# Second pairs of the second matrices in seven products on six input tiles, with two weight sums by adding transfers

## The chip, the core and the metric

One core of a Trainium2 chip. The time is the device time of one execution, in microseconds. A profiled execution leaves a trace of every instruction on each engine: PE (TensorE), DVE (VectorE), ACT (ScalarE), POOL (GpSimd), and SP, which only issues transfers. The matmuls' weight loads appear as a row of their own, PEld.

## What is computed

A trunk of two layers on 256 tokens of width 2048, in float32. Layer one: norm, one projection to queries, keys, values and forget gates, attention with a decaying bias, output projection, then an MLP with squared ReLU. Layer two takes shared keys and values from the residual stream, attends in chunks with a learned relative bias, and has an MLP of its own. The part that the change concerns above all is the MLP:

```python
def sq_relu_mlp(h, g, w1, w2):
    a = jax.nn.relu(rms_norm(h, g) @ w1)      # 2048 -> 8192
    return (a * a) @ w2                       # 8192 -> 2048
```

It is computed once in each layer, with h of 256 x 2048.

## The kernel before

**Units.** All weights stream from HBM once, as units of 128 x 1024 float32 (512 KB): two input tiles (of 128 rows) by 512 output columns. The token side stands on PE as 128 x 128 pieces, so a product of one input tile, 512 columns and 128 tokens is one matmul position. A float32 product is made from three passes of a shorter format. ACT rounds a unit to a high part (`hi`, line 184), DVE subtracts it to get the low part (`lo`, line 185), and PE adds high times high (line 408), high weight times low token part (line 410) and low weight times high token part (line 412). A plain unit is 2 input tiles x 2 token blocks x 3 passes = 12 matmuls.

**Queues.** Each engine works its instructions in the order in which the program writes them (`keep_order` at the end fixes it for DVE, ACT, PE and SP). `load` issues the transfer of a unit on SP into one of four `raw` buffers; `issue` writes its split on ACT and DVE; `fetch` keeps three split units ahead of PE and three loaded ones ahead of these. `hi` and `lo` have three buffers each. Everything else, such as transposes, norms, softmax and ReLU, is put in small steps into `fill`, one list of steps being run after each plain unit.

**Pairs.** An MLP is cut into four chunks of 2048 hidden columns. In each, two pairs of the first matrix and two of the second are computed; a pair is two panels (a and b) of 512 output columns over 16 input tiles. The first four input tiles of a pair are done with seven products instead of eight: with the two token blocks and the two panels they form a 2 x 2 by 2 x 2 product of blocks, and Strassen's method in Winograd's form needs seven block products on sums of blocks. The four weight blocks are called 11, 12, 21 and 22; the sums T1 = 12 - 11, T3 = 22 - 12, T2 = T3 + 11 and T4 = 21 - T2 are made on DVE from units in SBUF (`make`, line 760). The sums on the token side (`sums`, line 230) are made once for each input of a pair. The seven products, called forms f0 to f6, use 11, T3, T2, T1, 21, T4 and 22 in this order (`class Form`), 6 matmuls each (`form_products`). Copies and additions in PSUM (lines 837, 845, 853, 856) bring the partial results to where the remaining twelve plain units of the pair, a2 to a7 and b2 to b7, go on adding. Forms and plain units alternate by a written plan (`plan_mlp`), the first three forms with b5, b6 and b7 of the pair before.

**Weights of a pair's forms.** `prepare` brings the four blocks by SP (`bring`, line 744) and makes T1 and T3 a stated number of plain units before the pair begins (`Pair.units`). The blocks live in the rooms that keys and values have in attention (tags k and v, two buffers each), T1 and T3 in the room of the attention bias (tag bias, two buffers of 128 x 1536); T2 takes 12's place and T4 takes 11's.

**Around the change.** The first products need part of x (`load_x`, line 72, four tiles a transfer) and the first weights. The forget gates are summed, written to DRAM (`cd`, line 695) and read back broadcast as the bias of the first attention (`decay_bias`, line 712), both issued by SP; the second attention reads its relative bias in `rel_bias`, line 889.

Of the kernel before, what the change touches and what calls it, by code (L numbers as in the profile page):

```python
# [31 lines left out]
REL = 384  # L32

# [13 lines left out]
def trunk(ctx: ExitStack, tc: tile.TileContext, xT, xr, gs, hg, bf, wgate, w_in, w_oa, w1a, w2a,  # L47
          w_kv, w_qb, w_ob, w1b, w2b, rel, out):
# [23 lines left out]
    def load_x(i):  # L72
        raw_x[i] = qkv.tile([P, GH, T], F32, name="xin", tag="kv"[i // 2], bufs=2)
        SY.dma_start(raw_x[i], xT[:, i * GH : (i + 1) * GH, :])
# [3 lines left out]
    load_x(0)  # L78

# [4 lines left out]
    ones = const.tile([P, T], F32, name="ones")  # L84
    V.memset(ones, 1.0)
    warm = ps_o.tile([P, 512], F32, name="pt", tag="po")
    for _ in range(11):
        TE.matmul(warm[:, :P], ones[:, :P], ones[:, :P], start=True, stop=True)
# [18 lines left out]
    class Form:  # L107

        def __init__(self, pair, i):
            self.pair, self.name = pair, ("11", "T3", "T2", "T1", "21", "T4", "22")[i]  # L110
# [8 lines left out]
    class Pair:  # L119
# [3 lines left out]
        def __init__(self, src, first, order, third):  # L123
            self.src = [[src[first + q * 8 + u] for u in range(8)] for q in range(2)]
            self.third, self.ps, self.t, self.room, self.units = third, None, {}, None, (9, 8, 7, 6, 5, 2)
            self.head = {"early": "a2 f4 a3 f5 b2 f6 b3 a4 b4 a5 a6 a7", "late": "a2 f4 a3 f5 b2 f6 b3 a4 a5 b4 a6 a7",
                         "": "a2 f4 a3 f5 a4 f6 a5 a6 a7 b2 b3 b4"}[order]

        def items(self, names):
            return [(self, "abf".index(i[0]), int(i[1])) for i in names.split()]  # L130

    def plan_mlp(w1, w2, tail):
        n, pairs = w1.shape[0] // NCH, []
        for c in range(NCH):
            for src, late in ((w1, ""), (w2, "late")):
                for q in range(2):
                    pairs.append(Pair(src, c * n + 16 * q, (late if pairs else "early") if q == 0 else "", len(pairs) % 2 == 0))
        pairs[0].units, pairs[1].units, pairs[2].units = (15, 13, 11, 8, 10, 8), (9, 8, 7, 6, 3, 2), (9, 8, 7, 6, 1, 2)
        plan, rest = [], [(tail, 0, u) for u in range(KT // UA - 3, KT // UA)]
        for p in pairs:  # L140
            f = p.items("f0 f1 f2 f3")
            plan += [f[0], rest[0], f[1], rest[1], f[2], rest[2], f[3]] + p.items(p.head)
            rest = p.items("b5 b6 b7")
        plan += rest
        units.extend(Form(p, i) if q == 2 else p.src[q][i] for p, q, i in plan)
        return plan
# [6 lines left out]
    plan_a = plan_mlp(w1a, w2a, tail_a)  # L153
# [5 lines left out]
    plan_b = plan_mlp(w1b, w2b, tail_b)  # L159
# [15 lines left out]
    def issue(parts=1):  # L175
        if not raws:
            load(parts)
        raw, cuts = raws.popleft()
        if not cuts:
            raw, cuts = raw.pair.t[raw.name], [slice(0, UN)]  # L180
        hi = wsp.tile([P, UN], F32R, name="hi")
        lo = wsp.tile([P, UN], F32R, name="lo")
        for c in cuts:
            S.activation(hi[:, c], raw[:, c], AF.Copy)  # L184
            V.tensor_tensor(lo[:, c], raw[:, c], hi[:, c].bitcast(F32), op=ALU.subtract)  # L185
        ready.append((hi, lo))

    def fetch(ahead=AHEAD, early=EARLY):
        while (units or raws) and len(ready) <= ahead:
            issue()  # L190
        while units and sum(1 for r in raws if r[1]) < early:
            load()
        return ready.popleft()
# [36 lines left out]
    def sums(a, fs):  # L230

        w = [wk.tile([P, 512], F32, name="sum", tag="wk") for _ in range(2)]

        def part(i):
            v = w[i // 2][:, i % 2 * 256 : i % 2 * 256 + 256].rearrange("p (g t) -> p g t", g=2)
            return v.rearrange("p g (i c) -> p g i c", i=4) if len(a[0][0].shape) == 4 else v

        V.tensor_tensor(part(0), a[1][0], a[1][1], op=ALU.add)
        V.tensor_tensor(part(1), part(0), a[0][0], op=ALU.subtract)
        V.tensor_tensor(part(2), a[0][0], a[1][0], op=ALU.subtract)  # L240
        V.tensor_tensor(part(3), a[0][1], part(1), op=ALU.subtract)
        hi, lo = ([fs[k][:, i * 512 : (i + 1) * 512] for i in range(2)] for k in range(2))
        for i in range(2):
            S.activation(hi[i], w[i], AF.Copy)
        yield
        for i in range(2):
            V.tensor_tensor(lo[i], w[i], hi[i].bitcast(F32), op=ALU.subtract)
        yield

    def split_turned(t, n, which, into, fs=None):  # L250
        x = acts.tile([P, 2, GH, T], F32R, name="act")
        y = qkv.tile([P, GH, REL], F32, name="bias")[:, :, :T]
# [45 lines left out]
    def turned(name="q"):  # L298
        z = qkv.tile([P, GH * T], F32, name="z")
        return z, qkv.tile([P, GH * T], F32, name=name, tag=name, bufs=2)  # L300


    LONG = ((0, 1, 3, 5, 9, 10, 13, 14), (0, 1, 3, 5, 11, 12), (0, 1, 3, 5, 9, 10), (0, 1, 3, 5, 9, 10))
    SHORT = ((3, 1, 2, 3, 6, 7, 9, 10), (4, 2, 3, 5, 10, 11), (1, 2, 3, 4, 9, 10), (0, 0, 1, 2, 4, 5))

    def next_x(n, r2, stats, which, into, kept=None, fs=None, then=None):
# [21 lines left out]
        def f(b, ps):  # L328
            add_h(b, ps)
            if b == NB - 1:  # L330
                step = steps(use)
                do = [rows, turn, lambda: way[0](), lambda: way[1](), step, step, step, step]
                items = [[] for _ in range(max(at) + 1)]
                for i, d in zip(at[: 6 if fs is None else 8], do):
# [18 lines left out]
    class RowStats:  # L353
# [27 lines left out]
        def spread(self):  # L381
            self.R = const.tile([P, T], F32, name="R")
            pr = ps_o.tile([P, 512], F32, name="pt", tag="po")
            rb = wk.tile([P, NB, P], F32, name="rb", tag="wk")
            for b in range(NB):
                V.tensor_scalar(rb[:, b], ones[:, :P], self.r[:, b : b + 1], None, op0=ALU.mult)
# [48 lines left out]
    def form_products(ps, hi, lo, x, fs, i):  # L435
        items = []
        for g in range(2):
            if i in (0, 4, 5):
                xp = [x[2 * g + (i > 0)][:, k, (i == 5) * P : (i == 5) * P + P] for k in range(2)]
            else:  # L440
                c = {3: 0, 2: 1, 1: 2, 6: 3}[i] * 256 + g * P
                xp = [fs[k][:, c : c + P] for k in range(2)]
            items.append((ps[i not in (4, 5)][i in (1, 5)], xp, g, i < 2 and g == 0, i < 2 and g == 1))
# [177 lines left out]
    def begin(u):  # L621
        if u == 0:
            load(2)
            load(2)
# [24 lines left out]
    wgr = const.tile([P, KT * H], F32, name="wgr")  # L649
    ct = {}  # L650

    def gates(x, st):
# [5 lines left out]
        def clear():  # L658
            G.memset(w.bitcast(F32), 0.0)

# [11 lines left out]
        c = const.tile([H, T], F32, name="gc")  # L672

        def logs():
# [14 lines left out]
            V.tensor_tensor_scan(c, ones[:H, :], z, 0.0, op0=ALU.mult, op1=ALU.add)  # L689
# [5 lines left out]
            SY.dma_start(ct["cd"], nct)  # L695
            yield

        def turn_c():
            pc = ps_o.tile([P, 512], F32, name="pt", tag="po")
            ct["cq"] = const.tile([P, NB, H], F32, name="cq")  # L700
            for b in range(NB):
# [5 lines left out]
                [step], [step], [step], [step], [], [turn_c]]  # L707

    def decay_bias(g, box):
        nb = qkv.tile([P, GH, REL], F32, name="bias")  # L710
        src = ct["cd"][g * GH : (g + 1) * GH, :]
        SY.dma_start(nb, src.unsqueeze(0).to_broadcast([P, GH, REL]))
# [10 lines left out]
    for g in range(NG):  # L723
# [12 lines left out]
        zk, k = turned("k")  # L736
        v = qkv.tile([P, NB, 512], F32, name="v")
# [4 lines left out]
    def bring(p, name):  # L742
        t = qkv.tile([P, UN], F32, name="w" + name, tag="kv"[name[1] == "2"], bufs=2)
        SY.dma_start(t, p.src[int(name[1]) - 1][int(name[0]) - 1])
        p.t[name] = t

    def make(p, name):
        t = p.t
        if name in ("T1", "T3"):
            if p.room is not None:  # L750
                t[name] = p.room[:, (name == "T3") * UN : (name == "T3") * UN + UN]
            else:
                t[name] = qkv.tile([P, GH * REL], F32, name="w" + name, tag="bias", bufs=2)[:, :UN]
        elif name == "T2":
            t[name] = t["12"]
        else:
            t[name] = t["11"]
        a, b, op = {"T1": ("12", "11", ALU.subtract), "T3": ("22", "12", ALU.subtract),
                    "T2": ("T3", "11", ALU.add), "T4": ("21", "T2", ALU.subtract)}[name]
        V.tensor_tensor(t[name], t[a], t[b], op=op)  # L760

    def prepare(p, d):
        if d == p.units[0] and p.units[0] > 9:
            p.room = prob.tile([P, 9 * 3 * P], F32, name="wTT", tag="p", bufs=1)
        for name, at in zip(("12", "11", "22", "21", "T1", "T3"), p.units):
            if d == at:
                (make if name[0] == "T" else bring)(p, name)

    def mlp(plan, x, Sx, st, last):
# [4 lines left out]
        def take(t, c, n):  # L774
# [14 lines left out]
            if c or n:  # L789
                low()  # L790
                yield
            if n == 0:
                room = prob.tile([P, 9 * 3 * P], F32R, name="Sh", tag="p", bufs=1)
                Sh[c].extend(room[:, i * GH * T : (i + 1) * GH * T] for i in range(2))
                yield from sums([[t3[:, 2 * j + b :: 4] for j in range(2)] for b in range(NB)], Sh[c])
                if not c:
                    low()
                    yield

        def turn_hidden(c, n, late):  # L800
            zt = []

            def f(b, ps):
                if b == 0:
                    zt.extend(turned())
                blocks32(ps, zt[0], b)
                if b == NB - 1:
                    step = steps(lambda: take(zt[1], c, n))
                    uses = (4, 5, 6, 6 if late else 7) if n % 2 else (4, 5, 7, 8, 9, 10)[: 6 if n == 0 else 4]
                    if not c and n < 2:  # L810
                        uses = (5, 6, 7, 8) if n else (4, 5, 6, 7, 8, 10)
# [5 lines left out]
        def open_pair(p):  # L817
# [6 lines left out]
            else:  # L824
                p.evac = [turn_hidden(c, 2 * r + q, r == 1) for q in range(2)]

        starts = [i for i, it in enumerate(plan) if it[1:] == (2, 0)]
        for i, (p, q, u) in enumerate(plan):
            hi, lo = fetch()
            if p.ps is None:  # L830
                open_pair(p)
            if q == 2:
                form_products(p.ps, hi, lo, p.x, p.fs, u)
                if u == 0:
                    make(p, "T2")
                if u == 2:
# [138 lines left out]
```

## Time and profile before

| what | before |
|---|---|
| median of 3 runs | 2109.74 us (2108.97 to 2109.75) |
| the profiled execution, its own time | 2109.01 us |
| its span, first to last instruction | 2107.2 us |
| granted TensorE clock, mean | 1.000 |
| matmuls | 9332 |
| read from HBM | 450.01 MB |
| transfers under SP's queue | 489.96 MB, 71.2% of 16 engines' span |

The span is what the trace covers; the time has about 1.8 us around it. Busy times are of one engine; several work at once, so they don't add up to the span. A row of the groups reads: line, engine, operation, output and inputs, shapes, count, then total busy time and mean duration in ns, then the idle time before the group and what ended it. A row of the timeline reads: start, duration, engine, line, operation, count, and in brackets how long the engine had been idle and who released it.

### The profile page before, as it was taken

What the parts mean: (1) busy time and instruction counts of PE and PEld (TensorE: products, weight loads), DVE (VectorE), ACT (ScalarE), POOL (GpSimd) and SP (SyncE); (2) the same over time, 40 slices, a digit from 0 to 9 for tenths busy, and PEclk for the clock granted to TensorE, in tenths of its full rate; (3) what the DMA queues carried; (4) which work ended last, traced back from release to release, by engine and by line L of the source; (5) the groups of instructions that cost most, each with busy time, mean ns of one, the idle gap of its engine ahead of it and who ended that gap; (6) DMA issues with size and microseconds to landing.
All of it is one profiled execution on the core that took longest, in us unless ns stands there. A gap on an engine that the chain in (4) does not pass through costs nothing.

```text
span 2107.2 us, 26036 instructions
## 1 busy us (share of the span) xinstructions
PE 2099.1 (100%) x9332; PEld 1741.2 (83%) x9332; DVE 1587.3 (75%) x1812; ACT 1191.4 (57%) x1431; POOL 48.7 (2%) x47
## 2 busy tenths in 40 slices
PE   9999999999999999999999999999999999999999
PEld 8788888888888888888888888888888888888887
DVE  6777676887788777778767677678877877887775
ACT  6545455665466565556575455456654654665653
POOL 1001000000000000000001000000000000000000
PEclk9999999999999999999999999999999999999999
DMA  8787778776676676577678777787766666766774
GB/s 289 236 257 231 234 250 272 241 238 231 216 241 212 211 250 230 188 245 259 194 242 259 238 233 233 227 279 240 257 227 202 232 230 217 236 216 210 244 239 146
DMA packets 182594, 491.63 MB, mean 233 GB/s; under 512 B 36784, under 2 KB 74048, under 8 KB 182464
## 3 DMA queue, kind: packets, MB, share of 16 engines
q1 hardware_dynamic: 182464, 489.96, 71.2%
q8 instruction: 73, 1.20, 0.2%
q14 instruction: 57, 0.47, 0.1%
HBM read 450.01 MB, written 39.87 MB: 232 GB/s over the span
## 4 chain that ended last, share of the span: by engine, by line
PE 99%; DMA 1%; SPq 0%; ACT 0%; DVE 0%; issue 0%; DVEq 0%; ACTq 0%
PE acc L408 26%; PE acc L410 26%; PE acc L412 26%; PE s L408 6%; PE s L412 6%; PE s L410 6%; DMA raw<-in_w_in 1%; PE po L581 1%; PE s L550 1%; PE po L582 0%; PE s L549 0%; PE s L670 0%; DMA turn<-z 0%; SPq L294 0%; ACT hi L184 0%
## 5 line engine op out<-in xcount | busy, mean ns | idle before, releaser
L185 DVE TENSOR_TENSOR lo<-raw,hi 128x1024 fp32r<-128x1024 f32 (+1 forms) x642 | 778.3, 1216 | 296.8 <-ACT hi L184 286.5
L184 ACT ACTIVATE hi<-raw 128x1024 fp32r<-128x1024 f32 (+1 forms) x642 | 677.6, 1057 | 515.2 <-PE acc L410 394.7
L408 PE MATMUL acc<-hi,act 128*128 128x512 f32 x2306 | 632.9, 393 | 2.9 <-ACT hi L184 2.9
L410 PE MATMUL acc<-hi,act 128*128 128x512 f32 x2306 | 623.8, 389 | 0.0
L412 PE MATMUL acc<-lo,act 128*128 128x512 f32 x2306 | 623.5, 389 | 0.0
L410 PEld LDWEIGHTS acc<-hi,act 128*128 128x128 f32 x2306 | 432.8, 188 | 90.4
L412 PEld LDWEIGHTS acc<-lo,act 128*128 128x128 f32 x2306 | 432.8, 188 | 89.9
L408 PEld LDWEIGHTS acc<-hi,act 128*128 128x128 f32 x2306 | 430.8, 188 | 90.9 <-ACT hi L184 3.8
L184 ACT ACTIVATE hi<-w 128x1024 fp32r<-128x1024 f32 x160 | 169.5, 1059 | 153.8 <-PE acc L410 94.4
L185 DVE TENSOR_TENSOR lo<-w,hi 128x1024 fp32r<-128x1024 f32 x160 | 194.8, 1218 | 69.3 <-ACT hi L184 68.3
L408 PE MATMUL s<-hi,act 128*128 128x512 f32 x448 | 121.1, 389 | 0.0
L410 PE MATMUL s<-hi,act 128*128 128x512 f32 x448 | 121.0, 389 | 0.0
L412 PE MATMUL s<-lo,act 128*128 128x512 f32 x448 | 121.0, 389 | 0.0
L184 ACT ACTIVATE hi<-wT 128x1024 fp32r<-128x1024 f32 x60 | 63.6, 1059 | 62.1 <-PE acc L410 41.6
L410 PEld LDWEIGHTS s<-hi,act 128*128 128x128 f32 x448 | 84.1, 188 | 17.5
L412 PEld LDWEIGHTS s<-lo,act 128*128 128x128 f32 x448 | 84.1, 188 | 17.5
L408 PEld LDWEIGHTS s<-hi,act 128*128 128x128 f32 x448 | 84.0, 188 | 17.4
L185 DVE TENSOR_TENSOR lo<-wT,hi 128x1024 fp32r<-128x1024 f32 x60 | 73.2, 1220 | 28.0 <-ACT hi L184 27.8
L760 DVE TENSOR_TENSOR wT<-w,w 128x1024 f32<-128x1024 f32 x60 | 73.1, 1218 | 0.0
L584 ACT ACTIVATE act<-po 128x256 fp32r<-128x256 f32 x32 | 12.3, 385 | 91.1 <-PE po L582 91.1
L492 POOL TENSOR_TENSOR rn<-vv,mhalf 128x4 f32<-128x4 f32 x32 | 43.3, 1366 | 389.9 <-DVE vv L491 389.7
L585 DVE TENSOR_TENSOR act<-po,act 128x256 fp32r<-128x256 f32 x32 | 13.6, 425 | 51.3 <-ACT act L584 51.3
(164 smaller groups left out, 1347.7 us busy)
## 6 DMA issues: line engine op xcount, KB each, us to landing
raw<-in_w_in SPq DMA_DIRECT2D x96, 512.0 KB, 4.5
raw<-in_w1a SPq DMA_DIRECT2D x96, 512.0 KB, 4.3
raw<-in_w2a SPq DMA_DIRECT2D x96, 512.0 KB, 4.4
raw<-in_w1b SPq DMA_DIRECT2D x96, 512.0 KB, 4.3
raw<-in_w2b SPq DMA_DIRECT2D x96, 512.0 KB, 4.3
raw<-in_w_kv SPq DMA_DIRECT2D x64, 512.0 KB, 4.5
turn<-z SPq DMA_DIRECT2D x60, 512.0 KB, 4.2
q<-turn SPq DMA_DIRECT2D x168, 128.0 KB, 3.9
```

What stands on the lines that cost most here:

```text
L184: S.activation(hi[:, c], raw[:, c], AF.Copy)
L185: V.tensor_tensor(lo[:, c], raw[:, c], hi[:, c].bitcast(F32), op=ALU.subtract)
L408: TE.matmul(ps[:, cols], xh, cut(hi, j), start=first, stop=False, **kw)
L410: TE.matmul(ps[:, cols], xl, cut(hi, j), start=False, stop=False, **kw)
L412: TE.matmul(ps[:, cols], xh, cut(lo, j), start=False, stop=last, **kw)
L492: G.tensor_tensor(rn, vv, mhalf, op=ALU.pow)
L550: TE.matmul(s[:, P : 3 * P], q[:, a, P:T], k[:, a], start=True, stop=True)
L581: TE.matmul(po[:, :T], v[:, 0, a * P : (a + 1) * P], pT[:, :2], start=True, stop=False)
L584: S.activation(o[i][:, 0], po[:, :T], AF.Copy)
L585: V.tensor_tensor(o[i][:, 1], po[:, :T], o[i][:, 0].bitcast(F32), op=ALU.subtract)
L760: V.tensor_tensor(t[name], t[a], t[b], op=op)
```

## The change

In the second pair of the second matrix of each chunk, eight pairs in all, the seven products cover six input tiles instead of four. Each weight block is then three tiles high: 128 x 1536, 768 KB, from arrays laid out for this by the host (`w2fa`, `w2fb`, with the remaining units in `w2sa`, `w2sb`). Each of its forms is computed in two items: f with 1024 columns of such a block (6 matmuls) and a half h with the other 512 (3 matmuls), which has split buffers of its own, one of each. The pair keeps ten plain units, a3 to a7 and b3 to b7. Token-side sums for the third tile are made from the second group of hidden columns.

All weight sums, in every pair, become additions; the signs move to the token-side sums and to the PSUM steps, of which there is one more copy in each pair. In the wide pairs T1 and T4 are no longer made on DVE: a transfer issued by POOL reads a block from HBM and adds it to the tile in SBUF (`put`). T2 takes T3's place, so one bias buffer is enough, and the bias room goes from two buffers to one; the rooms of keys and values grow to 1536 columns.

The order changes too. After a form, `top_up` splits the next unit after that form's PSUM copies are written, where before `fetch` did so ahead of the form. The times at which blocks are brought and sums made, and the slots of several fill steps, are set anew. The gates' small tiles share the bias room, their write and the loads of both biases move from SP to POOL, and x's first transfer is cut into one of two tiles, ahead of the first weights, and one of two tiles behind them.

```diff
+WIDE = UN + 512
...
     def load_x(i):
-        raw_x[i] = qkv.tile([P, GH, T], F32, name="xin", tag="kv"[i // 2], bufs=2)
-        SY.dma_start(raw_x[i], xT[:, i * GH : (i + 1) * GH, :])
+        raw_x[i] = qkv.tile([P, WIDE], F32, name="xin", tag="kv"[i // 2], bufs=2)[:, : GH * T].rearrange("p (a t) -> p a t", a=GH)
+        if i:
+            SY.dma_start(raw_x[i], xT[:, i * GH : (i + 1) * GH, :])
...
     load_x(0)
+    SY.dma_start(raw_x[0][:, :UA], xT[:, :UA, :])
...
+            own = {"early": "a2 F a3 F b2 F b3 a4 b4 a5 a6 a7", "": "a2 F a3 F a4 F a5 a6 a7 b2 b3 b4",
+                   "late": "a2 F a3 F b2 F b3 a4 a5 b4 a6 a7", "wide": "a3 F b3 F a4 F b4 a5 a6 a7"}[self.order].split()
...
+            src = [[None] * 3 + [w2s[10 * c + 5 * j + u] for u in range(5)] for j in range(2)]
+            pairs.append(Pair({k: w2f[4 * c + i] for i, k in enumerate(names)}, src, "wide", len(pairs) % 2 == 0, (7, 5, 6, 4, 3, 2), True))
...
+        hi = wsp.tile([P, n], F32R, name="hi" if n == UN else "hih", bufs=3 if n == UN else 1)
+        lo = wsp.tile([P, n], F32R, name="lo" if n == UN else "loh", bufs=3 if n == UN else 1)
...
+        if form and half == form.pair.wide:
+            if form.name == "T3":
+                make(form.pair, "T2")
+            elif form.name == "T2" and half:
+                put(form.pair, "T4")
...
+    def top_up(ahead=AHEAD, early=EARLY):
+        while (units or raws) and sum(1 for r in ready if not r[2]) <= ahead and not (half_next() and any(r[2] for r in ready)):
             issue()
...
+    def room(tag, name, dtype=F32):
+        return qkv.tile([P, WIDE], dtype, name=name, tag=tag, bufs=1 if tag == "bias" else 2)
...
-    def form_products(ps, hi, lo, x, fs, i):
+    def form_products(ps, hi, lo, x, fs, i, half, stop):
         items = []
-        for g in range(2):
+        for g in (2,) if half else range(2):
...
-            SY.dma_start(ct["cd"], nct)
+            G.dma_start(ct["cd"], nct)
...
-        SY.dma_start(nb, src.unsqueeze(0).to_broadcast([P, GH, REL]))
+        G.dma_start(nb, src.unsqueeze(0).to_broadcast([P, GH, REL]))
...
+    def put(p, name):
+
+        at, other = {"T1": ("12", "11"), "T4": ("T2", "21")}[name]
+        p.t[name] = p.t[at]
+        G.dma_start(p.t[name][:, :WIDE], p.big[other], accum_op=ALU.add)
...
         for i, (p, q, u) in enumerate(plan):
-            hi, lo = fetch()
+            hi, lo = ready.popleft()[:2] if q > 1 and ready else fetch()
...
+            if q > 1:
+                form_products(p.ps, hi, lo, p.x, p.fs, u, q == 3, 1 + p.wide)
+                if u == 1 and q == 2 + p.wide:
+                    p.t["P7"] = wk.tile([P, 512], F32, name="p7", tag="wk")
+                    S.activation(p.t["P7"], p.ps[1][0], AF.Copy)
+                    S.activation(p.ps[1][0], p.ps[1][1], AF.Copy, scale=-1.0)
+                elif u == 2 and q == 2 + p.wide:
+                    V.scalar_tensor_tensor(p.ps[0][1], p.ps[1][0], -1.0, p.t["P7"], op0=ALU.mult, op1=ALU.subtract)
+                if q == 2 + p.wide:
+                    top_up(AHEAD - 1)
...
-        SY.dma_start(rb[:, :, :T], src)
+        G.dma_start(rb[:, :, :T], src)
```

More of the change, by code (lines that the diff above doesn't have):

```diff
@@ L87, in trunk @@
     for _ in range(11):
-        TE.matmul(warm[:, :P], ones[:, :P], ones[:, :P], start=True, stop=True)
+        TE.matmul(warm[:, :P], ones, ones, start=True, stop=True)
     mhalf = const.tile([P, GH], F32, name="mhalf")
@@ L179, in issue @@
         if not cuts:
-            raw, cuts = raw.pair.t[raw.name], [slice(0, UN)]
-        hi = wsp.tile([P, UN], F32R, name="hi")
-        lo = wsp.tile([P, UN], F32R, name="lo")
+            form, half = raw, raw.half
+            raw, cuts = form.pair.t[form.name], [slice(0, 512 if half else UN)]
+            if half:
+                raw = raw[:, UN:]
+        n = cuts[-1].stop
+        hi = wsp.tile([P, n], F32R, name="hi" if n == UN else "hih", bufs=3 if n == UN else 1)
+        lo = wsp.tile([P, n], F32R, name="lo" if n == UN else "loh", bufs=3 if n == UN else 1)
         for c in cuts:
@@ L440, in form_products @@
             else:
[L441 to L443 removed]
+                c = {3: 0, 2: 1, 1: 2, 6: 3}[i]
+                c = c * P if half else c * 256 + g * P
+                xp = [fs[k + 2 * half][:, c : c + P] for k in range(2)]
+            items.append((ps[i not in (4, 5)][i in (0, 5)], xp, g % 2, i < 2 and g == 0, i < 2 and g == stop))
         passes(items, hi, lo, skip_group_check=True)
@@ L647, in head_gains @@
         yield
-    wgr = const.tile([P, KT * H], F32, name="wgr")
+    early = room("bias", "early")
+    wgr = early[:, : KT * H]
     ct = {}
@@ L942 @@
     rel = np.zeros((H, REL), np.float32)
+    low = [_cols_a(i["mlp_w2"][j], True).reshape(NCH, 32, P, UN)[:, :16].reshape(-1, P, UN) for j in range(2)]
+    wide = [[a.reshape((NCH, 2, -1) + a.shape[1:])[:, 1].reshape((-1,) + a.shape[1:]) for a in _wide(i["mlp_w2"][j])] for j in range(2)]
     rel[:, REL - i["b_rel"].shape[2] :] = i["b_rel"][0]
@@ L959 @@
         "w1b": _cols_a(i["mlp_w1"][1], True),
[L960 removed]
+        "w2b": low[1],
+        "w2fb": wide[1][0],
+        "w2sb": wide[1][1],
         "rel": rel,
```

217 lines of the change are left out of this document (114 added, 103 removed).

## The prediction

> **What bounds the kernel now.** I read the page first: its span, its busy times, the chain of waits.
>
> ```profile
> span 2107.2 us, 26036 instructions
> PE 2099.1 (100%) x9332; PEld 1741.2 (83%) x9332; DVE 1587.3 (75%) x1812; ACT 1191.4 (57%) x1431; POOL 48.7 (2%) x47
> GB/s 289 236 257 231 234 250 272 241 238 231 216 241 212 211 250 230 188 245 259 194 242 259 238 233 233 227 279 240 257 227 202 232 230 217 236 216 210 244 239 146
> PE 99%; DMA 1%; SPq 0%; ACT 0%; DVE 0%; issue 0%; DVEq 0%; ACTq 0%
> ```
>
> PE is the bound, and the view of PE's own waits shows hardly any left:
>
> ```profile
> PE acc L408 <- ACT hi L184: 2.9, 2, 1.6
> PE pt L88 <- DVE mhalf L90: 1.2, 1, 1.2
> ```
>
> So time is won only by fewer matmuls, and lost by whatever makes PE wait. What a matmul costs is not its duration. The groups by shape give 389 ns, but 9332 of those would be 3630 us, more than the span: matmuls overlap. The rate is read from starts, here in the second pair of a second matrix:
>
> ```profile
> L412 PE MATMUL acc<-lo,act 128*128 128x512 f32 x2302 | 622.7, 389 | 0.0
> ```
>
> ```profile
> 499.36 1.07 PE L408 MATMUL acc<-hi,act 128*128 128x512 f32 x4
> ...
> 502.08 0.62 PE L408 MATMUL acc<-hi,act 128*128 128x512 f32 x2
> ...
> 503.44 1.07 PE L408 MATMUL s<-hi,act 128*128 128x512 f32 x4
> ...
> 506.16 0.62 PE L408 MATMUL acc<-hi,Sh 128*128 128x512 f32 x2
> ...
> 507.07 0.62 PE L412 MATMUL acc<-lo,Sh 128*128 128x512 f32 x2
> ...
> 507.52 1.07 PE L408 MATMUL s<-hi,act 128*128 128x512 f32 x4
> ...
> 510.24 0.62 PE L408 MATMUL acc<-hi,Sh 128*128 128x512 f32 x2
> ...
> 511.15 0.62 PE L412 MATMUL acc<-lo,Sh 128*128 128x512 f32 x2
> ...
> 511.60 1.07 PE L408 MATMUL s<-hi,act 128*128 128x512 f32 x4
> ...
> 511.83 0.69 DVE L837 TENSOR_TENSOR acc<-acc,p 128x512 f32<-128x512 f32 x1
> ```
>
> A plain unit (12 matmuls) runs from 499.36 to 502.08, 2.72 us; a form (6) from 502.08 to 503.44, 1.36 us: 0.2267 us a matmul. Forms start at 502.08 (f0), 506.16 (f1), 510.24 (f2), each followed by a plain unit (r0, r1, r2). These are the clocks against which every new wait is measured.
>
> **1. Fewer matmuls.** A pair on four input tiles takes 7 forms of 6 and 12 plain units of 12: 186. On six it takes 7 forms of 6, 7 halves of 3 and 10 plain units: 183. Four chunks in two layers give 8 such pairs: 24 matmuls less, 9308 in all, 24 x 0.2267 = **-5.4 us**. By the 389 ns it would be 9.3; the starts decide.
>
> **2. The start.** The first transfer of x carries two tiles instead of four before the first weights.
>
> ```profile
> 1.16 0.43 SPq L74 DMA_DIRECT2D xin<-in_xT  x1
> ...
> 5.28 0.91 ACT L226 ACTIVATE act<-xin,gsb 128x256 fp32r<-128x256 f32 x2 [3.06 <-DMA xin<-in_xT]
> ...
> 6.50 1.15 ACT L184 ACTIVATE hi<-raw 128x512 fp32r<-128x512 f32 x2 [0.31 <-DMA raw<-in_w_in]
> ...
> 7.18 0.73 PE L408 MATMUL acc<-hi,act 128*128 128x512 f32 x2 [1.33 <-ACT hi L184]
> ```
>
> 256 KB at the 289 GB/s of the first slice are 0.9 us. PE waited 1.33 us, which is the most that can be won; nothing if the weights don't come earlier. I take **-0.7**.
>
> **3. ACT and DVE work.** Durations, from the groups by shape:
>
> ```profile
> L185 DVE TENSOR_TENSOR lo<-raw,hi 128x1024 fp32r<-128x1024 f32 x638 | 775.8, 1219 | 296.3 <-ACT hi L184 286.0 <-PE acc L410 4.6 <-DMA q<-turn 2.9
> L184 ACT ACTIVATE hi<-raw 128x1024 fp32r<-128x1024 f32 x638 | 675.3, 1060 | 514.9 <-PE acc L410 394.7 <-PE s L410 76.7 <-DMA raw<-in_w_in 14.7
> L185 DVE TENSOR_TENSOR lo<-raw,hi 128x512 fp32r<-128x512 f32 x4 | 2.6, 686 | 0.5 <-ACT hi L184 0.5
> L184 ACT ACTIVATE hi<-raw 128x512 fp32r<-128x512 f32 x4 | 2.3, 620 | 0.3 <-DMA raw<-in_w_in 0.3
> L760 DVE TENSOR_TENSOR wT<-w,w 128x1024 f32<-128x1024 f32 x60 | 73.1, 1218 | 0.0
> L853 ACT ACTIVATE acc<-s 128x512 f32<-128x512 f32 x16 | 9.3, 582 | 0.0
> ```
>
> ```profile
> 502.00:544.20 42.20, 42.20 (x188) 34.96 (x187) 32.48 (x31) 21.19 (x22) 0.00 (x0) 1.00 0.59 199
> ```
>
> In a wide pair DVE does 17 low parts of 1.22, 7 half ones of 0.69 and two weight sums, 29.1 us with a 1536-column sum at 1.75 (1.22 plus the 0.53 that 512 columns add); before it was 23 x 1.22 = 28.1. ACT does 17 x 1.06 + 7 x 0.62 = 22.4 after 20.1, and one more 0.58 copy in every pair. The window over that pair (columns PE, PEld, DVE, ACT, POOL, clock, DMA share, GB/s) has DVE busy 32.5 and ACT 21.2 of 42.2 us, so on the average PE covers it: **0**. Uncovered, it would be up to 1.0 us of DVE a pair, 8 us.
>
> **4. The order at the second form.** This is the one new wait in all 32 pairs. The high part of f2 now stands on ACT behind two copies that need f1's last matmul; its low part and all later splits queue behind it on ACT and DVE. A form's result is there 0.23 us after the next unit starts (511.60, DVE at 511.83). So: f1 is over at 507.52, copies from 507.75, two of 0.58 to 508.91, high part to 509.97, low part to 511.19. PE wants the high part at 510.24 and the low part at 511.15. That is late by 0.04; in a wide pair both sides move by the half's 0.68 and the gap stays. Consecutive ACT instructions overlap a little, hand-overs cost a little: from 0 to some 0.3 us a pair, 0 to 9.6 us. I take 0.05: **+1.6**. The subtraction at f2 similarly puts f3's low part behind f2's end on DVE, but r2's 2.72 us cover it.
>
> **5. The adding transfers.** In each wide pair two sums, T1 and T4, leave DVE for POOL's queue, 768 KB each, added in SBUF. POOL has nothing else in these windows (0.00 above), so nothing queues behind them there. The trace has no adding transfer; the nearest rows:
>
> ```profile
> raw<-in_w2a SPq DMA_DIRECT2D x96, 512.0 KB, 4.4
> ...
> w<-in_w2b SPq DMA_DIRECT2D x32, 512.0 KB, 5.3
> ...
> bias<-cd SPq DMA_DIRECT2D x4, 768.0 KB, 6.7
> ```
>
> T1 starts when T3 is made, two plain units before the pair, and is wanted after r1: two plain units, f0 and h0, r0, f1 and h1, r1 lie between, 15 us, covered. T4 is the tight one. It may start when the low part of T2's half is made, some 6.4 us after f1 starts (f1 and its half over at 2.04, the copies done at 3.4, f2's high part at 4.5 and low part at 5.7, the half's low part 0.69 later). f5 starts 19.0 us after f1 (f1 and its half h1 2.04; r1 2.72; f2, h2 2.04; r2 2.72; f3, h3 2.04; a3 2.72; f4, h4 2.04; b3 2.72), and wants its high part, 1.06, before. That leaves 19.0 - 1.06 - 6.4 = 11.5 us; past it, ACT stands at f5's high part and PE waits for all that is late. Lower bound of the transfer: the 4.4 us of a plain one; upper: two reads of 768 KB one after the other, 13.4. I take the middle, some 9 us: **0**. The extra 1.57 MB over 41 us raise this pair's 199 GB/s to some 237, which the page shows elsewhere at no cost to PE.
>
> The Trainium skill, "Collectives: The Full Stack", section "The bandwidth ceiling: the fold count and why AG ≠ RS ≠ AR", says an add inside the DMA path is slow because it needs two source reads, so that its rate is half a copy's. By it the upper bound is the right one, and this term +15; no row here shows an adding transfer, so it is rival A.
>
> **6. What moves from SP to POOL, and single buffers.** The bias loads of attention and the write of the gate sums now issue from POOL, and the bias room has one buffer.
>
> ```profile
> 66.82 0.31 SPq L695 DMA_DIRECT2D cd<-nct  x1
> ...
> 69.60 0.32 SPq L712 DMA_DIRECT2D bias<-cd  x1
> ...
> 75.87 0.69 DVE L714 TENSOR_TENSOR bias<-bias,tri 128x512 f32<-128x512 f32 x1 [0.86 <-DMA bias<-cd]
> ...
> 85.19 1.20 PE L408 MATMUL acc<-hi,act 128*128 128x512 f32 x4 [1.60 <-ACT hi L184]
> ```
>
> SP stood between the two for the first's landing, with weight loads behind it, and PE lost 1.60 us at 85.19. On POOL this wait holds up no weights: as good as -1.6; but a later bias load holds up DVE, which already waited 0.86: as bad as +2. I take **0**. In the second attention the next bias may load only when the last softmax of the group before has read it, four units (10.9 us) before DVE copies from it; a load is 6.7.
>
> **Sum.** The profiled execution took 2109.0 (span 2107.2 and 1.8 around it); 2109.0 - 5.4 - 0.7 + 1.6 = **2104.5**. The median of the runs is 0.7 above this execution and inside their spread; I say 2104.6.
>
> **Rivals.**
> A: the adding transfer of T4 is late. For it: two operands to read, weights flowing at 199 GB/s beside it. Against: 16 rings that are only 0.59 busy. It decides from 11.5 us on; at 13.4 it is 1.9 us in each of 8 pairs, 15.2 more than the sum: **2119.7**, slower.
> B: the order at f2 costs 0.2 us or more in all 32 pairs, 6.4 instead of 1.6: **2109.3**, no change. For it: the margin of -0.04. Against: PE's waits of before were none in any form.
> C: the waits at 85 us and at f2 both vanish: 2109.0 - 5.4 - 0.7 - 1.6 = **2101.3**.
> That it doesn't remove the matmuls can be excluded only by the count: 9308.
>
> **How the numbers follow.** Forecast 0.47, A 0.25, B 0.17, C 0.11. A measurement here tells 0.2%, 4.2 us, from no change. Faster: C, and 0.85 of the forecast's case, whose own range is 2102.5 to 2106.5: 0.51. Same: the rest of it and half of B, 0.16. Slower: A and the other half of B, 0.33. The range for 8 in 10 goes from 2100.8 to 2121, leaving out A's upper part (longer landings) and C's lower.
>
> **What would show it.** PE's count 9308 and the total of its waits (4.1 us before): near 2 us in forms right, 14 or more wrong. A wait of PE on ACT's high part where ACT waited for the adding transfer is A; one of 0.1 to 0.3 at f2 in every pair is B. The landing time of the adding transfers stands in the DMA issues: under 11.5 right. The first product near 6.5 us instead of 7.18 shows step 2; the stall near 85, step 6. Wrong altogether would be waits in the plain units of a wide pair: weight loads held up on the DMA rings, which I have priced at nothing.

## The result, and the profile after

The kernel got slower: 2120.34 us (median of six runs, 2118.36 to 2122.53) against 2109.14 us for the kernel before on the same chip. The ratio is 1.0053, with a 95% interval from 1.0040 to 1.0066. The profiled execution took 2118.36 us, so it is the fastest of the six; it is 9.4 us above the profiled execution of before. What the other runs lose beyond it, up to 4 us, no trace shows.

The page of the kernel after, its span and its busy times:

```profile
span 2116.6 us, 26079 instructions
PE 2105.2 (99%) x9308; PEld 1731.8 (82%) x9308; DVE 1589.2 (75%) x1876; ACT 1217.5 (58%) x1511; POOL 68.4 (3%) x73
```

The 24 matmuls are gone (9332 to 9308), and yet PE is busy for 6.1 us longer. So busy time isn't what to read here: matmuls start 0.2267 us apart and are listed with 0.39 us on the average, so one that starts late but before its predecessor has ended leaves no idle time. PE's own waits therefore show only a part of the loss:

```profile
PE s L451 <- DVE acc L884: 3.4, 8, 0.4
PE acc L455 <- DVE lo L211: 1.4, 1, 1.4
```

The waits of the weight loads (the line, what released it; us in all, times, longest) point to two places that were not in the profile before, both in the products with pairs:

```profile
PEld s L455 <- DVE lo L211: 7.5, 24, 0.3
PEld acc L455 <- DVE lo L211: 7.3, 18, 1.8
PEld s L451 <- ACT acc L902: 6.6, 8, 0.8
```

How much time this is, the count of matmuls in a fixed stretch tells. The two stretches below hold the two MLPs and nothing else (columns PE, PEld, DVE, ACT and POOL busy, each with its count; clock; DMA share; GB/s). Before:

```profile
340.00:1064.00 724.00, 724.00 (x3196) 599.68 (x3195) 569.60 (x558) 431.67 (x475) 0.00 (x0) 1.00 0.70 232
1387.00:2096.00 709.00, 709.00 (x3130) 587.27 (x3129) 554.95 (x541) 415.92 (x443) 0.00 (x0) 1.00 0.69 229
```

After:

```profile
340.00:1064.00 724.00, 721.97 (x3162) 591.42 (x3161) 567.73 (x587) 439.00 (x506) 6.92 (x8) 1.00 0.71 236
1387.00:2096.00 709.00, 707.27 (x3097) 579.17 (x3097) 555.53 (x572) 426.87 (x482) 6.80 (x8) 1.00 0.71 237
```

In the same time, at the same granted clock (1.00), PE started 34 and 33 matmuls fewer: 67 x 0.2267 = 15.2 us. PE busy fell by only 3.8 us. The starts themselves, taken one by one (every start that comes more than 0.2267 us after the one ahead of it, the excess summed up), give the table to which the experiments below refer. Excesses under 0.005 us are left out, which makes these sums a little smaller than the count, and each is good to about 0.05 us:

| waits of PE, us | 66 to 93 us (first attention) | first MLP | second MLP |
|---|---|---|---|
| before | 2.28 | 0.00 | 0.00 |
| after | 2.09 | 7.20 | 6.92 |
| e1_order | 4.79 | 1.91 | 1.31 |
| e2_sums | 4.28 | 4.71 | 4.58 |
| e3_both | 4.70 | 2.59 | 0.34 |
| e5_sp | 1.30 | 1.73 | 0.93 |
| e7_early | 3.87 | 0.04 | 0.07 |
| e8_four | 2.09 | 0.19 | 0.06 |
| e9_all | 1.06 | 0.04 | 0.05 |

The 14.1 us of the two MLPs after are 0.20 us at f2 in each of the 32 pairs (6.4), 0.85 us at f3 in the first pair of a second matrix, eight times (6.8), and two single waits (0.6 and 0.3). With the matmuls that is 14.1 - 5.4 = 8.7; the spans differ by 9.4 us (2116.6 - 2107.2), so 0.7 is left for all other places.

One such first pair in the timeline of the kernel after (start, duration, engine and line; the brackets at the end give an idle time and what ended it). Forms start at 633.91 (f1), 637.99 (f2) and 642.86 (f3):

```profile
633.91 0.62 PE L451 MATMUL s<-hi,Sh 128*128 128x512 f32 x2
...
635.47 0.60 ACT L881 ACTIVATE p<-s 128x512 f32<-128x512 f32 x1 [2.52 <-PE s L455]
...
636.60 1.05 ACT L210 ACTIVATE hi<-wT 128x1024 fp32r<-128x1024 f32 x1
...
637.68 1.22 DVE L211 TENSOR_TENSOR lo<-wT,hi 128x1024 fp32r<-128x1024 f32 x1 [3.84 <-ACT hi L210]
...
637.99 0.62 PE L451 MATMUL s<-hi,Sh 128*128 128x512 f32 x2
...
638.96 0.74 PE L455 MATMUL s<-lo,Sh 128*128 128x512 f32 x2
639.54 1.09 PE L451 MATMUL acc<-hi,act 128*128 128x512 f32 x4
...
639.96 0.28 DVE L277 TENSOR_TENSOR sum<-q 128x128 f32<-128x128 f32 x1
...
640.69 0.28 DVE L280 TENSOR_TENSOR sum<-q,sum 128x128 f32<-128x128 f32 x1
...
640.89 1.22 DVE L801 TENSOR_TENSOR w<-w,wT 128x1024 f32<-128x1024 f32 x1
...
642.03 0.69 DVE L884 SCALAR_TENSOR_TENSOR acc<-s,p 128x512 f32<-128x512 f32 x1
...
642.86 0.70 PE L451 MATMUL s<-hi,Sh 128*128 128x512 f32 x2 [0.39 <-DVE acc L884]
```

and PE's weight loads in the same stretch:

```profile
637.77 0.41 PEld L451 LDWEIGHTS s<-hi,Sh 128*128 128x128 f32 x2
...
638.96 0.30 PEld L455 LDWEIGHTS s<-lo,Sh 128*128 128x128 f32 x2 [0.32 <-DVE lo L211]
```

The reader sees two waits with one origin. The split of f2 stands on ACT behind the two copies from PSUM (the first is shown), which wait for f1's last matmul; so f2's high part starts at 636.60, and its low part is ready at 638.90 (637.68 + 1.22). First, that is too late for f2. The matmul that uses it was due at 638.90 (637.99 + 4 x 0.2267), but the low part is loaded as a weight, and a load starts 0.22 us ahead of its matmul (637.77 and 637.99). This load starts at 638.96 instead of some 638.68, after an idle time of 0.32, and f2 takes 1.55 us (637.99 to 639.54) instead of 1.36: 0.19 lost.

Second, DVE, which has no work of its own in that time, stands idle for 3.84 us and then has everything at once: two low parts (the first is shown), the four sums for the third tile (the first and the last of them are shown), the weight sum T4 (L801), and only then the subtraction at f2 (L884, over at 642.72). The third form accumulates into the tile that this subtraction reads. It was due at 642.26 (639.54 + 2.72) and starts at 642.86, 0.60 late; its own low part, behind the subtraction, costs the rest of the 0.85. The weight-load row above names ACT's copy L902 instead; that copy (641.86 to 642.44) was over before the subtraction, which ended the wait.

### The profile page after: what moved, and what is told of

Its sections match the earlier page's. It is cut to its first block, busy times and chain, and to the rows that moved or that the text cites. A ratio compares the mean times of both kernels' runs of the same rounds, so it can differ in the third digit from the quotient of the medians.

```text
span 2116.6 us, 26079 instructions
## 1 busy us (share of the span) xinstructions
PE 2105.2 (99%) x9308; PEld 1731.8 (82%) x9308; DVE 1589.2 (75%) x1876; ACT 1217.5 (58%) x1511; POOL 68.4 (3%) x73
## 4 chain that ended last, share of the span: by engine, by line
PE 96%; DVE 2%; DMA 1%; issue 1%; ACT 1%; SPq 0%; DVEq 0%
PE acc L455 25%; PE acc L451 25%; PE acc L453 25%; PE s L455 6%; PE s L451 6%; PE s L453 6%; PE s L594 1%; PE po L625 1%; DVE lo L211 1%; DVE w L801 0%; DMA nb<-cd 0%; ACT hi L210 0%; PE s L593 0%; PE po L626 0%; DVE acc L884 0%
## 5 line engine op out<-in xcount | busy, mean ns | idle before, releaser
L211 DVE TENSOR_TENSOR lo<-raw,hi 128x1024 fp32r<-128x1024 f32 (+1 forms) x626 | 758.5, 1214 | 259.1 <-ACT hi L210 253.8
L210 ACT ACTIVATE hi<-raw 128x1024 fp32r<-128x1024 f32 (+1 forms) x626 | 660.1, 1055 | 424.5 <-PE acc L453 299.1
L451 PE MATMUL acc<-hi,act 128*128 128x512 f32 x2242 | 616.8, 393 | 1.4 <-ACT hi L210 1.1
L455 PE MATMUL acc<-lo,act 128*128 128x512 f32 x2242 | 606.7, 389 | 1.4 <-DVE lo L211 1.4
L453 PE MATMUL acc<-hi,act 128*128 128x512 f32 x2242 | 607.2, 389 | 0.0
L455 PEld LDWEIGHTS acc<-lo,act 128*128 128x128 f32 x2242 | 420.6, 188 | 89.6 <-DVE lo L211 2.2
L453 PEld LDWEIGHTS acc<-hi,act 128*128 128x128 f32 x2242 | 420.6, 188 | 88.9 <-DVE act L265 0.5
L451 PEld LDWEIGHTS acc<-hi,act 128*128 128x128 f32 x2242 | 418.6, 188 | 88.2 <-ACT hi L210 1.9
L211 DVE TENSOR_TENSOR lo<-w,hi 128x1024 fp32r<-128x1024 f32 x152 | 184.2, 1212 | 43.9 <-ACT hi L210 43.9
L211 DVE TENSOR_TENSOR lo<-wT,hi 128x1024 fp32r<-128x1024 f32 x72 | 87.9, 1220 | 97.4 <-ACT hi L210 97.4
L210 ACT ACTIVATE hi<-wT 128x1024 fp32r<-128x1024 f32 x72 | 76.0, 1055 | 44.4 <-PE acc L453 20.7
L801 DVE TENSOR_TENSOR wT<-w,w 128x1024 f32<-128x1024 f32 (+1 forms) x32 | 43.3, 1353 | 12.1 <-DMA w<-in_w2fb 6.3
```

Of the source, the lines that this page charges most:

```text
L451: TE.matmul(ps[:, cols], xh, cut(hi, j), start=first, stop=False, **kw)
L453: TE.matmul(ps[:, cols], xl, cut(hi, j), start=False, stop=False, **kw)
L455: TE.matmul(ps[:, cols], xh, cut(lo, j), start=False, stop=last, **kw)
L801: V.tensor_tensor(d, a, b, op=ALU.add)
```

## Experiments

All ratios are against the kernel before, on the same chip, with their 95% intervals. The numbers to compare them with are 1.0000 (before) and 1.0053 (after). The kernel before itself took 2109.14 us beside the kernel after, 2107.71 beside e1 to e4 and 2108.42 beside e5 to e9, so gains between these groups are read from the ratios, not from the medians.

**e1_order: the split of f2 ahead of the copies.** Nothing else changes; ACT makes f2's high part while f1 still runs.

```diff
                 if u == 1 and q == 2 + p.wide:
+                    top_up(AHEAD - 1)
                     p.t["P7"] = wk.tile([P, 512], F32, name="p7", tag="wk")
...
-                if q == 2 + p.wide:
+                if u != 1 and q == 2 + p.wide:
                     top_up(AHEAD - 1)
```

> The changed kernel with one edit: at the second form the next unit's split is written ahead of the two PSUM copies instead of behind them. Theory (order on ACT): the wait of some 0.20 us before the third pass of f2 in all 32 pairs goes, 6.4 us, to about 2114; the wait of 0.85 us before f3 in the eight first pairs of the second matrices stays. Rival (the adding transfers are what costs): nothing changes, 2120. Second rival: f2 then waits for the copies instead, and the gain is under 2 us.

Measured: 2106.73 us, ratio 0.9995 (0.9986 to 1.0005). One edit of order takes 0.0058 off the ratio, some 12 us. It took more than was expected of it (6.4 us): the wait at f2 went, and the wait at f3 went with it. The same pair in the timeline of e1_order:

```profile
634.97 1.06 ACT L210 ACTIVATE hi<-wT 128x1024 fp32r<-128x1024 f32 x1 [0.30 <-PE acc L453]
...
635.63 0.61 PE L451 MATMUL s<-hi,Sh 128*128 128x512 f32 x2
...
636.07 1.22 DVE L211 TENSOR_TENSOR lo<-wT,hi 128x1024 fp32r<-128x1024 f32 x1 [0.51 <-ACT hi L210]
...
639.71 0.61 PE L451 MATMUL s<-hi,Sh 128*128 128x512 f32 x2
...
642.61 0.69 DVE L885 SCALAR_TENSOR_TENSOR acc<-s,p 128x512 f32<-128x512 f32 x1
...
643.79 0.61 PE L451 MATMUL s<-hi,Sh 128*128 128x512 f32 x2
```

DVE makes f2's low part 0.44 us after f1 starts (in the kernel after 3.77), so it uses the time in which it had stood idle. The subtraction is over at 643.30, and f3 starts on its clock at 643.79, 4.08 us after f2 at 639.71.

**e2_sums: the token sums of the third tile two plain units later.** This takes the four small sums out of the crowd ahead of the subtraction and leaves the order at f2 alone.

```diff
-                    uses = ((4, 5, 7, 8, 9, 10, 11), (4, 5, 6, 7, 11, 12, 13), (4, 5, 7, 8), (4, 5, 6, 6))[n]
+                    uses = ((4, 5, 7, 8, 9, 10, 11), (4, 5, 6, 7, 13, 14, 15), (4, 5, 7, 8), (4, 5, 6, 6))[n]
...
-                        uses = (5, 6, 7, 8, 11, 12, 13) if n else (4, 5, 6, 7, 8, 9, 10)
+                        uses = (5, 6, 7, 8, 13, 14, 15) if n else (4, 5, 6, 7, 8, 9, 10)
```

> The changed kernel with one edit: the token-side sums for the third tile run two plain units later, behind the forms of the first pair of the second matrix and not between them. Theory (DVE stands in these sums and T4 when the subtraction at f2 is due, and f3 waits for that subtraction): the wait of 0.85 us before f3 goes in eight pairs, 6.8 us, to about 2113.5; the 0.20 us at f2 stay. Rival (adding transfers): 2120. Second rival (T4 alone is enough to hold up the subtraction): under 3 us are won.

Measured: 2112.69 us, ratio 1.0027 (1.0017 to 1.0037). The row of PE's waits on L884 is gone, and 0.2 us at f2 in the pairs stays: the MLPs wait 9.3 us, down from 14.1. All eight waits at f3 are gone; what is left beside the 6.4 at f2 is of another kind, the largest (0.9 and 1.0 us) at 1012 and 1553 us, where ACT had stood for 7.1 us ahead of the first split of a wide pair. So the sums are the last load on DVE that makes f3 wait, and the order at f2 is a loss without them too.

**e3_both: e1 and e2 together.**

> Both edits together. Theory: the two waits are separate and add up, 13 us, to about 2107, and PE in the MLPs is left with under 1.5 us of waits; then the 24 matmuls less are seen as some 5 us against the matmul time of the kernel before, less what start and attention cost. Rival (adding transfers): 2120.

Measured: 2107.47 us, ratio 0.9999 (0.9990 to 1.0008). The number is as expected, the reasoning behind it isn't: the two gains don't add, as e1 alone already had both. The MLPs still wait 2.9 us, where under 1.5 was expected. Their one large wait is of the other kind, ACT without a weight block:

```profile
1008.38 1.06 ACT L210 ACTIVATE hi<-w 128x1024 fp32r<-128x1024 f32 x1 [7.10 <-DMA w<-in_w2fa]
```

In e1_order ACT waits like this too. The view of waits over all engines:

```profile
ACT hi L210 <- DMA w<-in_w2fa: 24.9, 4, 6.6
ACT hi L210 <- DMA w<-in_w2fb: 19.2, 3, 6.7
...
DVE nb L761 <- DMA nb<-cd: 8.2, 1, 8.2
```

These lines gave the next experiments: the plain loads of the wide pairs (e7), and the bias load that now issues from POOL (e5).

**e4_dve: no adding transfers.** T1 and T4 of the wide pairs are made by DVE, as they are in the other pairs.

```diff
-            pairs.append(Pair({k: w2f[4 * c + i] ...}, src, "wide", len(pairs) % 2 == 0, (7, 5, 6, 4, 3, 2), True))
+            pairs.append(Pair({k: w2f[4 * c + i] ...}, src, "wide", len(pairs) % 2 == 0, (7, 5, 6, 4, 3, 2)))
...
-            elif form.name == "T2" and half:
-                put(form.pair, "T4")
...
             elif done == 2:
                 S.activation(f.ps[0][0], f.ps[1][1], AF.Copy)
+                if f.wide:
+                    make(f, "T4")
```

> The changed kernel with T1 and T4 of the wide pairs made on DVE, T4 after the third form, and no adding transfers. Theory (the adding transfers land in time and cost PE nothing): 2120 as before the edit, within 2 us, and the scatter from run to run stays. Rival (the adding transfers are late or disturb the weight loads): about 2110 or less, and the runs scatter less.

Measured: 2136.44 us, ratio 1.0136 (1.0121 to 1.0151). Neither theory expected this. DVE has no room for these sums in the wide pairs at the times that this kernel gives it, and PE waits for DVE (its waits, the first two rows):

```profile
PE acc L449 <- DVE acc L888: 5.9, 8, 1.0
PE acc L453 <- DVE loh L211: 5.6, 7, 1.1
```

In this order the adding transfers are worth 0.0083 of the ratio (1.0136 - 1.0053), some 17.5 us. They are no cost here. How much of this e1's order would take away wasn't tried.

**e5_sp: e1, with the gate sums and the first attention's bias on SP again.**

```diff
-            G.dma_start(ct["cd"], nct)
+            SY.dma_start(ct["cd"], nct)
...
-        G.dma_start(nb, src.unsqueeze(0).to_broadcast([P, GH, REL]))
+        SY.dma_start(nb, src.unsqueeze(0).to_broadcast([P, GH, REL]))
```

> The kernel of e1_order with the write of the gate sums and the loads of the first attention's bias back on SP. Theory (on POOL the two transfers take longer, DVE stands 8 us for the bias and PE loses 4.5 us between 66 and 93 us, 2.3 before): 2 to 2.5 us less than e1_order's 2106.7, about 2104.4, and DVE's wait for the bias back to some 1 us. Rival (the stall there is the weights' traffic, whoever issues the bias): no change, 2106.7.

Measured: 2106.07 us, ratio 0.9989 (0.9980 to 0.9998). The time alone doesn't decide between theory (2104.4) and rival (no change): the ratio is 0.0006 below that of e1_order, some 1.3 us, and the intervals overlap. The traces speak against the rival: DVE's wait for the bias falls from 8.2 to 1.35, and PE's waits from 66 to 93 us from 4.79 to 1.30.

Those 4.79 are not what a usual execution of e1_order loses. Its trace is of the slowest of ten (2110.25 us), and in it the granted clock fell to half, from 84.85 us for 3.4 us, while PE waited for a late low part (until 85.10). The same stretch in e1_order and in e5_sp (columns as above; the clock is the third number from the end):

```profile
85.00:88.00 3.00, 2.90 (x9) 2.43 (x9) 3.00 (x5) 1.06 (x1) 0.00 (x0) 0.50 0.62 178
```

```profile
85.00:88.00 3.00, 3.00 (x15) 2.47 (x14) 2.92 (x3) 2.64 (x3) 0.00 (x0) 1.00 0.48 157
```

At half the clock matmuls start 0.427 us apart. The traces of e2_sums, e3_both and e7_early show a fall of the same length, which begins up to 1.5 us after such a wait; it makes 1.5 to 1.8 us of the waits of all four in the table's first column. In these four, PE had waited 2.0 to 3.0 us in one piece near 85 us; in the five other traces of the table the longest wait there was 1.8 us or less, and the clock stayed full. As far as these nine traces go, a late bias costs PE twice: the wait, and, when the wait is long, the slow matmuls behind it.

The write and the load in the timeline of e5_sp:

```profile
67.26 0.31 SPq L742 DMA_DIRECT2D cd<-nct  x1
...
70.00 0.32 SPq L759 DMA_DIRECT2D nb<-cd  x1
...
77.31 0.69 DVE L761 TENSOR_TENSOR nb<-nb,tri 128x512 f32<-128x512 f32 x1 [1.35 <-DMA nb<-cd]
```

and in that of the kernel after:

```profile
67.25 0.70 POOL L742 DMA_DIRECT2D cd<-nct  x1 [5.70 <-DVE nct L740]
...
72.37 0.58 POOL L759 DMA_DIRECT2D nb<-cd  x1 [4.42 <-PE acc L455]
...
81.43 0.69 DVE L761 TENSOR_TENSOR nb<-nb,tri 128x512 f32<-128x512 f32 x1 [7.00 <-DMA nb<-cd]
...
83.31 1.21 PE L455 MATMUL acc<-lo,act 128*128 128x512 f32 x4 [1.35 <-DVE lo L211]
```

The bias is issued 2.4 us later and lands later, so DVE starts on it 4.1 us later; behind it DVE's low parts are late for PE.

**e7_early: e1, with the wide pairs' blocks one plain unit earlier.** It is an edit of the numbers that say how many units ahead a block is brought.

```diff
-            ... "wide", len(pairs) % 2 == 0, (7, 5, 6, 4, 3, 2), True))
+            ... "wide", len(pairs) % 2 == 0, (8, 6, 7, 5, 3, 2), True))
```

> The kernel of e1_order with the four blocks of a wide pair brought one plain unit earlier each. Theory (the 768 KB blocks land in 8.3 us, later than ACT wants the first, and now and then PE waits): ACT's 24 us of waiting for them in each layer go, the few waits of PE before wide pairs go, 1 to 2 us less than e1_order, about 2105.2. Rival (ACT's waiting is all covered, PE's waits there have other reasons): 2106.7.

Measured: 2104.27 us, ratio 0.9982 (0.9973 to 0.9990). The MLPs' waits fall from 3.2 us to 0.1. ACT no longer stands for the blocks of the wide pairs, so here the due times of plain loads, not the adding ones, were too short. The ratio is 0.0013 below that of e1_order, some 2.7 us; the two intervals just overlap.

**e8_four: e1, with the second pairs of the second matrices on four tiles, as before.** This takes back what the change is about and leaves its order, its queues and its buffers. The blocks of these pairs, and of the pairs that follow them, also come earlier, at the due times of the other four-tile pairs (9, 7, 8, 6, 5, 2). The token sums of a third tile are still made, though no form uses them.

```diff
-            src = [[None] * 3 + [w2s[10 * c + 5 * j + u] for u in range(5)] for j in range(2)]
-            pairs.append(Pair({k: w2f[4 * c + i] for i, k in enumerate(names)}, src, "wide", len(pairs) % 2 == 0, (7, 5, 6, 4, 3, 2), True))
+            src = [[w2[32 * c + 16 + 8 * j + u] for u in range(8)] for j in range(2)]
+            pairs.append(Pair({k: src[int(k[1]) - 1][int(k[0]) - 1] for k in names}, src, "", len(pairs) % 2 == 0, (9, 7, 8, 6, 5, 2)))
```

> The kernel of e1_order with the second pairs of the second matrices back on four input tiles, their sums on DVE, no adding transfers (the third tile's token-side sums are still made, and not used). Theory (with the order put right the 24 matmuls less are worth their 5.4 us): about 5 us more than e1_order, 2111.5 to 2112. Rival (six tiles and their transfers give back what they save): 2106.7 or less.

Measured: 2109.59 us, ratio 1.0006 (0.9998 to 1.0015), with 9332 matmuls and 0.25 us of waits in the MLPs. Against e1_order that is 0.0011 of the ratio, some 2 us where about 5 were expected, as e1_order itself still waits 3.2 us in the MLPs. Against e7_early, measured beside it, whose MLPs wait as little (0.11), it is 5.3 us slower. That agrees with the 24 matmuls: 24 x 0.2267 = 5.4.

**e9_all: the edits of e1, e5 and e7.**

> e1_order with both edits, the bias on SP and the blocks earlier. Theory: the gains add, about 2103, 0.25% under the kernel before, PE's waits in the MLPs under 2 us in all. Rival: whatever one of the two does not give, up to 2106.7.

Measured: 2103.30 us, ratio 0.9976 (0.9968 to 0.9985): it beats both kernels, by 0.24% and 0.8%. Its page and its windows over the two MLPs:

```profile
span 2100.9 us, 26112 instructions
PE 2094.6 (100%) x9308; PEld 1735.8 (83%) x9308; DVE 1595.6 (76%) x1876; ACT 1223.5 (58%) x1511; POOL 66.3 (3%) x68
```

```profile
340.00:1064.00 724.00, 724.00 (x3195) 599.58 (x3194) 576.24 (x593) 447.61 (x515) 7.09 (x8) 1.00 0.72 240
1387.00:2096.00 709.00, 709.00 (x3131) 587.16 (x3130) 558.13 (x570) 429.54 (x482) 6.80 (x8) 1.00 0.70 235
```

PE starts 3195 and 3131 matmuls in these stretches, as many as before the change (3196 and 3130): the form with fewer matmuls now runs at full rate, with all of DVE's and ACT's added work. The steps of e9's gain, in ratios: after 1.0053, order 0.9995, loads earlier 0.9982, bias back on SP 0.9976. The first step is far beyond the intervals; of the other two, each by itself, the intervals overlap.

## Why the prediction was wrong, by its steps

The forecast of 2104.6 us, faster, was wrong by 15.7 us; the measured 2120.34 lies inside the stated range, which reached that far for another reason (rival A). That rival A's 2119.7 is so near the measured time is chance: what it said didn't happen.

**Step 4 is the one that failed, in two ways.** It named the right place, but took 0.05 us a pair, and PE loses 0.20 (0.18 to 0.23) in each, 6.4 us instead of 1.6. That part is a term mis-sized, and it is what rival B said. The working held the end of the low part against the start of its matmul, late by 0.04, and left out the weight load that stands 0.22 us ahead of the matmul; 0.04 + 0.22 = 0.26 is near the 0.20 measured. The timeline speaks for this reading; no run tested it by itself. The second part is a wrong step: "The subtraction at f2 similarly puts f3's low part behind f2's end on DVE, but r2's 2.72 us cover it." It looked for what queues behind the subtraction. It didn't ask what stands ahead of it on DVE, nor that f3 waits for the subtraction itself. Ahead of it, in a first pair of a second matrix, stand two low parts, the four new sums of the third tile and T4, all let go at once by ACT's late high part. e1 and e2 show it from both sides: with the order mended or with the sums away, the 6.8 us at f3 vanish.

**Step 1, right.** -5.4 was predicted; e8_four against e7_early shows 5.3. The rate read from starts (0.2267) holds; the listed 389 ns would have given 9.3.

**Step 2, right in mechanism, wrong in what it brings.** The first product starts earlier, by 0.86 us (7.18 before):

```profile
6.32 0.73 PE L451 MATMUL acc<-hi,act 128*128 128x512 f32 x2 [1.06 <-ACT hi L210]
...
52.24 0.94 PE L451 MATMUL acc<-hi,act 128*128 128x512 f32 x3
```

But the matmul that starts at 52.24 here, the 223rd in both traces, started at 52.10 before:

```profile
52.10 1.17 PE L408 MATMUL acc<-hi,act 128*128 128x512 f32 x4
```

In between PE waits again, in short pieces at 9.3, 12.2 and from 20.8 to 22.4 us, where its weight loads stand for ACT and DVE; so the -0.7 is lost.

**Step 3, right as a term, thin as a cover.** With the order and the due times mended, all of ACT's and DVE's added work costs nothing in the MLPs (e9_all, 0.1 us). e4_dve shows how near the edge DVE is.

**Step 5, right; rival A fell.** The issues of the kernel after (size, median us from issue to landing):

```profile
w<-in_w2fa SPq DMA_DIRECT2D x16, 768.0 KB, 8.4
w<-in_w2fb SPq DMA_DIRECT2D x16, 768.0 KB, 8.1
nb<-cd POOLq DMA_DIRECT2D x4, 768.0 KB, 9.8
w<-in_w2fa POOLq DMA_DIRECT2D x4, 768.0 KB, 7.2
wT<-in_w2fa POOLq DMA_DIRECT2D x4, 768.0 KB, 7.6
cd<-nct POOLq DMA_DIRECT2D x1, 24.0 KB, 4.4
```

The adding transfers (from POOL's queue; the first MLP's T1 and T4 are shown) landed after 7.2 and 7.6 us, inside the 11.5 that T4 had. ACT did stand for T4's landing, five times and up to 2.0 us, but PE's starts show no late one there. The Trainium skill, "Collectives: The Full Stack", section "The bandwidth ceiling: the fold count and why AG ≠ RS ≠ AR", says of the add in a ring collective that its two source reads halve the rate of a copy; the prediction took this for adding transfers in general. These rows, of single transfers, don't show it: plain loads of the same size, issued by SP, took 8.1 to 8.4. They run on another queue and at other moments; a plain 512 KB load on POOL's queue, the second attention's bias, took 7.8. So no factor of two is seen here, which doesn't show that adding is free.

**Step 6, taken as 0, is a loss once the order is mended, of some 1 us as far as the runs tell.** It went the way of the upper end, "as bad as +2". In the kernel after itself it doesn't show in PE's total (2.09 us of waits against 2.28 before), though DVE's wait went from 0.86 to 7.00. Bringing the bias back to SP took 1.3 us by the ratios of e1_order and e5_sp and 1.0 us by the medians of e7_early and e9_all, each inside its interval. The traces of e1_order and e5_sp differ by 3.5 us there, 1.5 of it by the clock of the one execution.

Two things stay open. The profiled execution of the kernel after is the fastest of its six, and what the others lose no trace shows; a fall of the clock as in e1_order may be part of it, since the slowest of them has a mean clock of 0.999 (one such fall makes 3.4 x 0.5 us in some 2100). And with the same instructions there the bias lands at different times: PE's wait near 84 us was 1.5 us in the kernel after, 3.0 in e1_order and 2.0 in e7_early. Why, no run tells.

## What to carry to other kernels

Work that doesn't depend on a wait belongs ahead of it on an in-order engine. An order that puts it behind costs twice: on that engine, and on the one fed by it, which stands idle first and then has too much to do; ask what has to be done ahead of each result, not only what queues behind it. Where the bound engine's instructions overlap, count its starts in a fixed stretch instead of its busy time, and judge a saving only when the order around it is mended: with the same 24 matmuls less the time was +0.5% as first arranged, and -0.24% once the order, the due times and the bias's queue were mended.

## What the hardware showed that was not expected

The matmul rows alone don't show what a late weight costs. The one at 638.96 is only 0.06 us behind its clock, and is listed with 0.74 us instead of the 0.62 of its neighbours; the form behind it is 0.19 late. Thirty-two such places make 6.4 us, of which PE's own list of waits shows nothing.

A wait of PE of 2.0 us or more near 85 us was followed by 3.4 us at half the granted clock (e1_order, above). Among all executions with the bias on POOL, the kernel after and e1 to e4, e7 and e8, 21 of 61 have a mean clock of 0.999; of the 22 with the order mended and the bias on SP (e5_sp, e9_all) none has, and of the 57 of the kernel before beside them 4 have. Only the four traces show that such a mean is this fall.

The same transfers took longer when POOL issued them: the 768 KB bias load 9.8 us instead of 6.7 from SP, the 24 KB write of the gate sums 4.4 instead of 2.8. e1_order and e5_sp, which differ in the issuer alone, show the same: 10.1 and 7.4, 5.3 and 2.6. The row of the kernel before for the write:

```profile
cd<-nct SPq DMA_DIRECT2D x1, 24.0 KB, 2.8
```
